# Hybrid S5 / RG-LRU encoder block: chunk-matrix sums by accumulating transfers, first norm by halves, embedding results in half tiles

## The chip, the cores and the metric

The kernel runs on one core of one Trainium2 chip. The metric is the device time of one execution in microseconds (us). Engines are named as in the profile: PE is the matrix engine (PEld its weight loads), DVE the vector engine, ACT the scalar engine, POOL the GpSimd engine, SP the sync engine, which here does nothing but issue transfers. SBUF is the on-chip memory, PSUM the memory that PE writes into, DRAM the memory of the chip's stacks.

## The reference

All data are float32, with 1024 positions and 1024 channels. Cut to what matters:

```
u = rms_norm(x, g_mix)                              # the first norm
u_a, x_b, gate_b, merge_a, merge_b = split(u @ w_in)       # 5 x 1024 columns
y_a  = u_a * s5_d
for d in (forward, backward):                       # S5: 64 groups of 16 channels, 64 complex states
    y_a += Re(C . scan(lam_bar, B_bar . u_a))
branch_a = gated(gelu(y_a)) @ w_a_out
branch_b = (rglru(conv(x_b)) * gelu(gate_b)) @ w_b_out
h = x + (sigmoid(merge_a)*branch_a + sigmoid(merge_b)*branch_b) @ w_o
v = rms_norm(h, g_ffn);  h = h + (silu(v @ w_ff_gate) * (v @ w_ff_up)) @ w_ff_down
h = h + sigmoid(rms_norm(h, g_ple) @ w_ple_gate) * (p @ w_ple_proj)   # the layer's embedding p
return rms_norm(h, g_final)
```

## The kernel before

**Numbers.** Every large product is made of three: each operand is split into a high part and a low part (ACT rounds the high part, DVE subtracts it from the original), and PE forms high x high, high x low and low x high.

**Start.** Eight tiles `xt[0..7]`, 128 positions by 1024 channels each, are loaded. `norm_pair` (line 190) takes two of them: ACT squares each tile and sums it (line 194) and takes the root (line 195), DVE does a Newton step on a 128x2 strip (`rstd_newton`) and scales both tiles (line 198). After two pairs `transposed_half` turns four tiles by PE (line 208) into PSUM, and from there ACT writes the high parts `xh` with the gain (line 213) and DVE the low parts `xl` (line 214), 512 columns at a time. Then come the next two pairs and the second half. The first products with `w_in` (`pi_u`, line 159) need all eight `xh`, `xl` of a half.

**Tables.** `s5_tables` then works out on DVE what the S5 recurrence needs, PE and ACT rearrange it, and it is stored to DRAM as `tab`. The first stretch of the S5 stage begins when the first of it is loaded back (`tb`).

**S5 stage.** Sixteen steps of four groups each. `s5_step(hb)` runs `s5_mid(hb)` (two scans on DVE with carries between them), then for step hb+2 `s5_mats` and `s5_front`, then `s5_out(hb)`. `s5_mats` builds two matrices of 128x1024 by `gen` (line 499): DVE forms two products into `t` and `u` (line 503) and adds them (line 505); `t` is called `mo` once and `mt` once, `u` is `mu`, a single buffer. From both PE forms `pk` (lines 516 and 519); ACT and DVE make the small tile `kt` of it, which goes through DRAM (`kk`, then `mr`) and comes back as `m0`. PE also transposes `mt` (`pmi`, line 536), ACT copies it to `mi` (line 538), and `s5_front` uses `mi` as weights for `pS` (line 551). `s5_out` needs `m0`, `mo` and the state `X` (`py`, lines 625 to 627). POOL issues no transfer; it only clears small strips of `carry`, `dzf` and `X` (lines 580, 583, 613).

**Fillers.** Beside the S5 steps stand projections: `inproj` is 48 products of 128x512 (line 159) for one block of 128 columns of `w_in`, one after most steps and two after every fourth. The twelve that are left come after the S5 stage, in the RG-LRU stage.

**Order.** Each engine runs its instructions in a fixed order. A planner sets that order when the program is built, from the order in the text (`tc.high_priority` moves a piece forward) and its own estimate of each duration; semaphores do the rest at run time. So an engine that waits for one instruction holds up everything planned behind it. Buffers are shared by tag: `ot(...)` hands out three tiles of 128x1024 (tag `o`), `act` forty of 128x512, and the tag `vt` four of 128x512.

**Embedding.** `embed_proj(m)` (line 1171) multiplies the embedding with `w_ple_proj` into two PSUM banks; ACT copies both to one tile `prj` from `ot` (line 1181) and one transfer stores it as `prd[m]` (line 1182). Around it run the first five hidden blocks' `head_group`s, whose result tile `hd` is also from `ot`, and the first `hidden_group`, whose second weight tile `fu` is from `ot` as well (line 1115, loaded at line 1047). Its first operands `rs` are sums of that weight tile (lines 1071 and 1072).

Of the kernel before, what the change touches and what calls it, by code (L numbers as in the profile page):

```python
# [8 lines left out]
F32 = mybir.dt.float32  # L9
F32R = mybir.dt.float32r  # L10
I32 = mybir.dt.int32
AF = mybir.ActivationFunctionType
# [3 lines left out]
MUL, ADD, SUB, MAX, MIN = ALU.mult, ALU.add, ALU.subtract, ALU.max, ALU.min  # L16
# [37 lines left out]
def block_kernel(tc, a, out):  # L54
    nc = tc.nc
    V, A, T, G = nc.vector, nc.scalar, nc.tensor, nc.gpsimd
    dma = nc.sync.dma_start
# [5 lines left out]
    cp = ctx.enter_context(tc.tile_pool(name="const", bufs=1))  # L63
# [11 lines left out]
    def psb(name):  # L75
        return pb.tile([128, 1024], F32, name=name, tag="pb")

    def ot(name):
        return op.tile([128, 1024], F32, name=name, tag="o")
# [12 lines left out]
    warm = cp.tile([128, 1], F32, name="warm")  # L92
# [19 lines left out]
    def r1(name, dt=F32R):  # L112
        return r1p.tile([128, S], dt, name=name, tag="r1", bufs=16)

    xh = [r1(f"xh{k}") for k in range(KT)]
    xl = [r1(f"xl{k}") for k in range(KT)]
# [4 lines left out]
    def slot(name, dt=F32, shape=None):  # L121
        return sp.tile(shape or [128, 1024], dt, name=name, tag="s", bufs=NS)
# [43 lines left out]
    xt, first_w = [], []  # L166
    for j in range(8):
        t = slot(f"x{j}")
# [8 lines left out]
    ss = cp.tile([128, 8], F32, name="ss")  # L177
    rs = cp.tile([128, 8], F32, name="rs")
    nt = cp.tile([128, 8], F32, name="nt")

    def rstd_newton(y, sq, t):

        V.reciprocal(y, y)
        V.tensor_scalar(t, sq, 1.0 / D, EPS, MUL, ADD)
        V.tensor_tensor(t, t, y, MUL)
        V.tensor_tensor(t, t, y, MUL)
        V.tensor_scalar(t, t, -0.5, 1.5, MUL, ADD)
        V.tensor_tensor(y, y, t, MUL)

    def norm_pair(q):  # L190
        qs = slice(q * 2, q * 2 + 2)
        for j in range(q * 2, q * 2 + 2):
            junk = ot("junk")
            A.activation(junk, xt[j], AF.Square, bias=warm, accum_out=ss[:, j:j + 1])
        A.activation(rs[:, qs], ss[:, qs], AF.Sqrt, bias=epsc, scale=1.0 / D)
        rstd_newton(rs[:, qs], ss[:, qs], nt[:, qs])
        for j in range(q * 2, q * 2 + 2):
            V.tensor_scalar(xt[j], xt[j], rs[:, j:j + 1], None, MUL)

    def transposed_half(h):  # L200

        cs = slice(h * 512, h * 512 + 512)
        ks = range(KT) if h == 0 else range(2)
        for k0 in range(0, KT, len(ks)):
            pt = [(psm if h == 0 and i % 2 else psb)("ptx") for i in range(len(ks) // 2)]
            for j in range(4):
                for k in ks:
                    T.transpose(pt[k // 2][:, (k % 2) * 512 + j * 128:(k % 2) * 512 + (j + 1) * 128],
                                xt[h * 4 + j][:, (k0 + k) * 128:(k0 + k + 1) * 128], ident)
            for k in ks:  # L210
                src = pt[k // 2][:, (k % 2) * 512:(k % 2) * 512 + 512]
                g = gmix[:, k0 + k:k0 + k + 1]
                A.activation(xh[k0 + k][:, cs], src, AF.Identity, scale=g)
                V.scalar_tensor_tensor(xl[k0 + k][:, cs], src, g, xh[k0 + k][:, cs].bitcast(F32), MUL, SUB)

    pv = psb("pv")
    T.transpose(pv[:, :8], grow, ident[:8, :8])
    V.tensor_copy(gmix, pv[:, :8])
    for h in range(2):
        norm_pair(2 * h)  # L220
        norm_pair(2 * h + 1)
        first_w[h] = split(first_w[h], [128, 8, 128], f"u{h}")
        transposed_half(h)


    vrows = cp.tile([128, 128], F32, name="vrows")
# [246 lines left out]
    ps = psb("ps_d")  # L473
# [10 lines left out]
    def st5(name, bufs, shape=None):  # L484
        return s5p.tile(shape or [128, 1024], F32, name=name, tag=name, bufs=bufs)

    def s5_mats(hb):
        tb = tabp.tile([128, MATW], F32, name="tb", tag="tb", bufs=2)
        dma(tb, tab[hb][:, 0:MATW])
        rb = tabp.tile([128, TABW - MATW], F32, name="rb", tag="trb", bufs=3)  # L490
        dma(rb, tab[hb][:, MATW:])

        def v8(o):
            return tb[:, o:o + 64].rearrange("p (d k) -> p d k", d=8)

        def v16(o):
            return tb[:, o:o + 128].rearrange("p (d k) -> p d k", d=8)

        def gen(o1, o2, q1, q2, name):
            t = st5(name, 3 if name == "mo" else 1, [128, 8, 16, 8])  # L500
            u = st5("mu", 1, [128, 8, 16, 8])
            for dst, o, q in ((t, o1, q1), (u, o2, q2)):
                V.tensor_tensor(dst, v8(o).unsqueeze(2).to_broadcast([128, 8, 16, 8]),
                                v16(q).unsqueeze(3).to_broadcast([128, 8, 16, 8]), MUL)
            V.tensor_tensor(t, t, u, ADD)
            return t

        mo = gen(O_LA, O_LB, O_K1, O_K2, "mo")
        t = gen(O_T1, O_T2, O_B1, O_B2, "mt")

        k1 = v16(O_K1)
        pk = psb("pk")
        bq = [t[:, q, :, 7 * (q // 4)] for q in range(8)]
        for q in range(8):
            d = q // 4
            T.matmul(pk[0:16, q * 128:q * 128 + 112], bq[q], mo[:, q, :, d:d + 7], start=True, stop=True)
        for g in range(4):
            for q in (g, 4 + g):
                T.matmul(pk[0:16, g * 128 + 112:(g + 1) * 128], bq[q], k1[:, q, :], start=(q < 4), stop=(q >= 4))
        kt = tabp.tile([16, 15, 4, 16], F32, name="kt", tag="kt", bufs=1)  # L520
        pkv = pk[0:16].rearrange("p (q n) -> p q n", q=8)
        A.copy(kt[:, 8:15].rearrange("p m g h -> p g h m"), pkv[:, 0:4, 0:112].rearrange("p g (h m) -> p g h m", m=7))
        A.copy(kt[:, 0:7].rearrange("p m g h -> p g h m"), pkv[:, 4:8, 0:112].rearrange("p g (h m) -> p g h m", m=7))
        V.tensor_tensor(kt[:, 7], ident[0:16, 0:16].unsqueeze(1).to_broadcast([16, 4, 16]),
                        dcol[:, hb * 4:hb * 4 + 4].unsqueeze(2).to_broadcast([16, 4, 16]), MUL)
        V.tensor_tensor(kt[:, 7], kt[:, 7], pkv[:, 0:4, 112:128], ADD)
        kd = kkd[hb]
        dma(kd.rearrange("p m n -> p (m n)"), kt.rearrange("p m g h -> p (m g h)"))
        mr = tabp.tile([128, 8, 4, 16], F32, name="mr", tag="mr", bufs=1)

        dma(mr.rearrange("p i g h -> p (i g h)"), bass.AP(kd.tensor, kd.offset, [[960, 16], [64, 8], [1, 512]]))
        m0 = tabp.tile([128, 4, 16, 8], F32, name="m0", tag="m0", bufs=3)
        A.copy(m0, mr.rearrange("p i g h -> p g h i"))
        pt = psb("pmi")
        for dg in range(8):
            T.transpose(pt[:, dg * 128:(dg + 1) * 128], t[:, dg].rearrange("p h j -> p (h j)"), ident)
        mi = st5("mi", MI, [128, 8, 128])
        A.copy(mi.rearrange("p d n -> p (d n)"), pt)  # L538
        return rb, m0, mi, mo
# [266 lines left out]
    tabp = tabp_cm.__enter__()  # L806
# [47 lines left out]
    for m in range(8):  # L854
        w = wload(a["s5_glu_w"][0][:, m * 128:(m + 1) * 128], f"gl{m}")
        ps = psm("pgl")
        gemm(ps, w, [x[0] for x in gp], [x[1] for x in gp])
        with hp():
            t = ot("glt")
            A.activation(t, ps, AF.Sigmoid, bias=vcol("s5_glu_b", m))  # L860
            g = ot("glg")
# [9 lines left out]
    for m in range(8):  # L871
        w = wload(a["w_a_out"][0][:, m * 128:(m + 1) * 128], f"ao{m}")
        ps = psm("pao")
        gemm(ps, w, [x[0] for x in yp], [x[1] for x in yp])
        with hp():
            t = ot("ta")
# [12 lines left out]
    qp = ctx.enter_context(tc.tile_pool(name="qp", bufs=1, reuse_waits="tile"))  # L889
# [8 lines left out]
    def half(n):  # L898
        return slice(n * 512, n * 512 + 512)
# [8 lines left out]
    for m in range(8):  # L908
        w = wload(a["w_b_out"][0][:, m * 128:(m + 1) * 128], f"bo{m}")
        ps = psm("pbo")  # L910
        gemm(ps, w, [x[0] for x in bp], [x[1] for x in bp])
        h, l = pair(f"mh{m}", F32R), pair(f"ml{m}", F32R)
        with hp():
            t, u = ot("tb"), ot("br")
# [26 lines left out]
    prd = [dram(f"prd{m}", [128, 1024]) for m in range(8)]  # L941
# [229 lines left out]
    def embed_proj(m):  # L1171

        if m % 4 == 0:
            with hp(HPW):
                wpp[0] = wload(a["w_ple_proj"][0][:, m * 128:m * 128 + 512], f"pp{m}")
        ps = [bank("ppj"), bank("ppj")]
        gemm(ps, wpp[0], pth, ptl, ms=slice((m % 4) * 128, (m % 4 + 1) * 128))
        yield
        t = ot("prj")
        for n in range(2):  # L1180
            A.copy(t[:, half(n)], ps[n])
        dma(prd[m], t)
        yield

    for n in range(2):
        acc = qp.tile([128, 512], F32, name="acc", tag="acc", bufs=2)
        for m in range(8):
# [8 lines left out]
            h = hpart(m, n)  # L1196
            A.copy(h, pt)
            ps = bank("pwo")
# [56 lines left out]
    for ib, nb in enumerate(BLOCKS):  # L1255
        fh, fl = [], []
        for ht in range(h0, h0 + nb):
            h, l = pair(f"fh{ht}", F32R), pair(f"fl{ht}", F32R)
            with hp(HPD):
                t = ot("hid")  # L1260
# [4 lines left out]
        if ib + 1 < len(BLOCKS):  # L1265
            for m in range(8):
                w = wload(wd[h0 * 128:(h0 + nb) * 128, m * 128:(m + 1) * 128], f"fd{h0}_{m}")
                ps = [bank("pfd"), bank("pfd")]
# [7 lines left out]
    for k in range(8):  # L1276
        t = r1(f"uh{k}")
# [3 lines left out]
    for n in range(2):  # L1281
        acc = qp.tile([128, 512], F32, name="acc", tag="acc", bufs=2)
        cs = slice(n * 512, n * 512 + 512)
        for m2 in range(4):
            w = wload(wd[(h0 - nb) * 128:h0 * 128, m2 * 256:(m2 + 1) * 256], f"fe{n}_{m2}")
            for mm in range(2):
                m = m2 * 2 + mm
                ps = bank("pfd")
# [33 lines left out]
    for n in range(2):  # L1322
# [3 lines left out]
        for m in range(8):  # L1326
            w = wload(a["w_ple_gate"][0][:, m * 128:(m + 1) * 128], f"pg{n}{m}")
            with hp(HPW):
                prj = act("prj")
                dma(prj, prd[m][:, cs])  # L1330
            ps = bank("ppg")
# [5 lines left out]
            t = qp.tile([128, 512], F32, name="vt2", tag="vt", bufs=4)  # L1337
# [4 lines left out]
            q = qp.tile([128, 512], F32, name="sqf", tag="vt", bufs=4)  # L1342
# [39 lines left out]
```

## Time and profile before

| | us |
|---|---|
| three runs | 1907.79, 1908.8, 1911.62 |
| median | 1908.8 |
| the profiled execution, its own time | 1907.41 |
| its span (first to last instruction) | 1905.2 |
| PE busy | 1841.4 (97%) |
| DVE busy | 1315.1 (69%) |
| ACT busy | 909.7 (48%) |
| POOL busy | 7.8 (0%) |

The span is what the profile pictures; 2.2 us lie around it. Busy time is a mean over stages: a stage is read by its own stretch of the span. Waits are listed as "engine, line, what waited <- who released it: total us, times, longest us".

### The profile page before, as it was taken

Reading aid. Unit: us, or ns where it says so; the run is one execution under the profiler, and the core shown is the slowest. Engines: PE = TensorE matmul, PEld = TensorE weight load, DVE = VectorE, ACT = ScalarE, POOL = GpSimd, SP = SyncE. Lnnn points to the kernel's source line nnn. Section 1 sums busy time; section 2 is a strip of 40 time slices with the busy share of each in tenths; the row PEclk is TensorE's granted clock in tenths of the full one; section 3 lists DMA queues with packets and bytes.
Section 4 is the critical chain, followed back from the end, with each engine's and each line's share of the span. In section 5 each row is a group of like instructions: output and inputs, shape, how many; then the busy total and the mean of one; then the engine's idle time right before and its main releaser. Section 6 shows DMA issues by size and latency. Waiting matters only on the chain.

```text
span 1905.2 us, 23270 instructions
## 1 busy us (share of the span) xinstructions
PE 1841.4 (97%) x8997; PEld 1532.0 (80%) x8997; DVE 1315.1 (69%) x1810; ACT 909.7 (48%) x1238; POOL 7.8 (0%) x60
## 2 busy tenths in 40 slices
PE   7999889988999999999999999999999999999998
PEld 6787777777788888878888887888888888888887
DVE  7517999999534779797444677867777774343875
ACT  6675666656555687865223454223232332122543
POOL 0000000000000000000000000000000000000000
PEclk8999999999999999999999999999999999999999
DMA  4795343433233356565746645422222264322433
GB/s 146 194 234 151 112 128 119 131 115 109 97 111 99 129 193 211 164 210 179 230 134 180 184 166 188 145 76 91 76 92 74 93 217 130 96 83 67 139 111 127
DMA packets 285855, 263.48 MB, mean 138 GB/s; under 512 B 32688, under 2 KB 244784, under 8 KB 285744
## 3 DMA queue, kind: packets, MB, share of 16 engines
q1 hardware_dynamic: 285744, 261.99, 44.2%
q8 instruction: 71, 1.16, 0.3%
q14 instruction: 40, 0.33, 0.1%
HBM read 185.86 MB, written 76.09 MB: 137 GB/s over the span
## 4 chain that ended last, share of the span: by engine, by line
PE 68%; DVE 2%; DMA 1%; ACT 1%; issue 1%; DVEq 0%; ACTq 0%
PE q L1060 22%; PE pfd L159 13%; PE pwo L159 5%; PE ppg L159 5%; PE pi_a L159 5%; PE pgl L159 5%; PE pg L159 4%; PE pbo L159 4%; PE pi_b L159 3%; PE pao L159 2%; PE ppj L159 1%; DMA ld_yb<-ybd 1%; DMA brd<-ta 1%; PE pfin L1312 0%; PE pxr L1195 0%
## 5 line engine op out<-in xcount | busy, mean ns | idle before, releaser
L1271 DVE TENSOR_TENSOR h<-h,pfd 128x512 f32<-128x512 f32 x48 | 32.6, 684 | 113.3 <-PE pfd L159 113.3
L982 ACT CAST s<-rs 128x512 fp32r<-128x512 f32 x44 | 27.2, 618 | 148.4 <-DVE rs L1072 148.4
L159 PE MATMUL pfd<-fh,wh_fd 128*128 128x512 f32 x288 | 88.7, 389 | 0.0
L159 PE MATMUL pfd<-fl,wh_fd 128*128 128x512 f32 x288 | 88.7, 389 | 0.0
L159 PE MATMUL pfd<-fh,wl_fd 128*128 128x512 f32 x288 | 88.6, 389 | 0.0
L134 ACT CAST wh_fd<-ws_fd 128x768 fp32r<-128x768 f32 x24 | 20.1, 835 | 122.1 <-PE pfd L159 121.4
L1060 PE MATMUL q<-xt2h,s 128*128 128x512 f32 x176 | 59.2, 398 | 4.3 <-ACT s L982 3.9
L159 PEld LDWEIGHTS pfd<-fl,wh_fd 128*128 128x128 f32 x288 | 54.1, 188 | 11.3
L159 PEld LDWEIGHTS pfd<-fh,wh_fd 128*128 128x128 f32 x288 | 54.1, 188 | 11.2
L159 PEld LDWEIGHTS pfd<-fh,wl_fd 128*128 128x128 f32 x288 | 54.1, 188 | 11.2
L1060 PE MATMUL q<-xt3h,s 128*128 128x512 f32 x176 | 57.7, 389 | 0.0
L1060 PE MATMUL q<-xt1h,s 128*128 128x512 f32 x176 | 57.7, 389 | 0.0
L1060 PE MATMUL q<-xt4h,a 128*128 128x512 f32 x176 | 57.7, 389 | 0.0
L1060 PE MATMUL q<-xb1h,s 128*128 128x512 f32 x176 | 57.7, 389 | 0.0
L551 PE MATMUL pS<-U,mi 128*128 128x128 f32 x256 | 32.6, 281 | 22.6 <-ACT mi L538 22.6
L551 PEld LDWEIGHTS pS<-U,mi 128*128 128x128 f32 x256 | 29.7, 191 | 28.9 <-ACT mi L538 28.5
L159 PE MATMUL pwo<-mh,wh_wo 128*128 128x512 f32 x128 | 51.5, 402 | 0.0
L159 PE MATMUL ppg<-uh,wh_pg 128*128 128x512 f32 x128 | 50.8, 397 | 0.0
L159 PE MATMUL pwo<-mh,wl_wo 128*128 128x512 f32 x128 | 50.1, 392 | 0.0
L159 PE MATMUL ppg<-uh,wl_pg 128*128 128x512 f32 x128 | 49.9, 390 | 0.0
L159 PE MATMUL ppg<-ul,wh_pg 128*128 128x512 f32 x128 | 49.8, 389 | 0.0
L159 PE MATMUL pwo<-ml,wh_wo 128*128 128x512 f32 x128 | 49.8, 389 | 0.0
(544 smaller groups left out, 5362.9 us busy)
## 6 DMA issues: line engine op xcount, KB each, us to landing
ws_fg<-in_w_ff_gate_dram SPq DMA_DIRECT2D x22, 512.0 KB, 4.2
fu<-in_w_ff_up_dram SPq DMA_DIRECT2D x22, 512.0 KB, 4.0
hid<-up SPq DMA_DIRECT2D x22, 512.0 KB, 3.4
hid<-hid SPq DMA_DIRECT2D x22, 512.0 KB, 4.6
ws_fd<-in_w_ff_down_dram SPq DMA_DIRECT2D x24, 384.0 KB, 3.5
ws_wo<-in_w_o_dram SPq DMA_DIRECT2D x16, 512.0 KB, 5.0
ws_pg<-in_w_ple_gate_dram SPq DMA_DIRECT2D x16, 512.0 KB, 3.9
tb<-tab SPq DMA_DIRECT2D x16, 384.0 KB, 3.1
```

Source lines behind the costliest of these rows:

```text
L134: A.copy(wh, st)
L159: T.matmul(pn_[:, sub], ww[:, k0 + k, ms], xn[:, sub], start=(first and i == 0), stop=(last and i == tot - 1))
L551: T.matmul(pS[:, q * 128:(q + 1) * 128], mi[:, q, :], rhs, start=True, stop=True)
L982: A.copy(h, raw)
L1060: T.matmul(ps, ww[:, k], xx, start=i == 0, stop=i == 11)
L1271: V.tensor_tensor(hres[m][:, half(n)], hres[m][:, half(n)], ps[n], ADD)
```

## The change

Four things change together.

1. `gen` no longer adds `u` to `t` on DVE. POOL issues a transfer that adds `u` into `t` while it writes (`accum_op=ADD`), SBUF to SBUF, 128x1024 float32. There are two of them for each of 16 steps. `mu` gets a second buffer, and to make room `kt` moves from a buffer of its own to a tile of tag `o`.
2. The first norm goes by four tiles: two are squared on ACT, two on DVE (`tensor_tensor_reduce`), then one root and one Newton step on a 128x4 strip, and of four tiles DVE scales three and ACT one.
3. The squares of the second half take their zero from a tile that DVE computes from `xl[4]` of the first half, so they come after it.
4. `prj` becomes two tiles of 128x512 of tag `vt`, each stored by a transfer of its own.

```diff
-    def norm_pair(q):
-        qs = slice(q * 2, q * 2 + 2)
-        for j in range(q * 2, q * 2 + 2):
+    def norm_half(h, start):
+
+        qs = slice(h * 4, h * 4 + 4)
+        for j in range(h * 4, h * 4 + 4):
             junk = ot("junk")
-            A.activation(junk, xt[j], AF.Square, bias=warm, accum_out=ss[:, j:j + 1])
+            if j % 2:
+                V.tensor_tensor_reduce(junk, xt[j], xt[j], 1.0, start, MUL, ADD, ss[:, j:j + 1])
+            else:
+                A.activation(junk, xt[j], AF.Square, bias=start, accum_out=ss[:, j:j + 1])
         A.activation(rs[:, qs], ss[:, qs], AF.Sqrt, bias=epsc, scale=1.0 / D)
         rstd_newton(rs[:, qs], ss[:, qs], nt[:, qs])
-        for j in range(q * 2, q * 2 + 2):
-            V.tensor_scalar(xt[j], xt[j], rs[:, j:j + 1], None, MUL)
+        for j in range(h * 4, h * 4 + 4):
+            if j % 4 == 3:
+                A.mul(xt[j], xt[j], rs[:, j:j + 1])
+            else:
+                V.tensor_scalar(xt[j], xt[j], rs[:, j:j + 1], None, MUL)
...
+    zeros = [warm, cp.tile([128, 1], F32, name="zero2")]
...
     for h in range(2):
-        norm_pair(2 * h)
-        norm_pair(2 * h + 1)
+        norm_half(h, zeros[h])
         first_w[h] = split(first_w[h], [128, 8, 128], f"u{h}")
         transposed_half(h)
+        if h == 0:
+
+            V.tensor_scalar(zeros[1], xl[4][:, 0:1].bitcast(F32), 0.0, None, MUL)
...
-            u = st5("mu", 1, [128, 8, 16, 8])
+            u = st5("mu", 2, [128, 8, 16, 8])
...
-            V.tensor_tensor(t, t, u, ADD)
+
+            G.dma_start(out=t.rearrange("p a b c -> p (a b c)"), in_=u.rearrange("p a b c -> p (a b c)"), accum_op=ADD)
...
-        kt = tabp.tile([16, 15, 4, 16], F32, name="kt", tag="kt", bufs=1)
+        kt = ot("kt")[0:16, 0:960].rearrange("p (m g h) -> p m g h", m=15, g=4)
...
-        t = ot("prj")
         for n in range(2):
-            A.copy(t[:, half(n)], ps[n])
-        dma(prd[m], t)
+            t = qp.tile([128, 512], F32, name="prj", tag="vt", bufs=4)
+            A.copy(t, ps[n])
+            dma(prd[m][:, half(n)], t)
```

## Rows read from the trace of the kernel before

**Rows 1.** The page's head.
```profile
span 1905.2 us, 23270 instructions
```

**Rows 2.** Busy time by stretch; then granted PE clock, transfer engines' share, GB/s.
```profile
0.00:24.00 24.00, 14.33 (x88) 12.78 (x88) 13.76 (x41) 17.06 (x29) 1.24 (x14) 0.88 0.75 251
24.00:50.00 26.00, 26.00 (x119) 21.17 (x120) 23.85 (x107) 13.82 (x18) 0.00 (x0) 0.92 0.19 57
50.00:150.00 100.00, 98.43 (x507) 80.22 (x506) 31.81 (x92) 63.17 (x120) 0.25 (x3) 1.00 0.88 218
150.00:510.00 360.00, 323.61 (x2141) 277.63 (x2140) 332.52 (x369) 223.10 (x308) 6.35 (x43) 1.00 0.38 117
510.00:1150.00 640.00, 636.17 (x2839) 524.77 (x2838) 421.26 (x422) 350.53 (x377) 0.00 (x0) 1.00 0.52 166
1150.00:1200.00 50.00, 45.72 (x194) 37.13 (x193) 35.41 (x58) 16.00 (x29) 0.00 (x0) 0.97 0.70 220
...
```

**Rows 3.** Waits from 150 to 510 us.
```profile
POOL X L613 <- PE py L627: 130.9, 14, 9.5
...
ACT rosw L481 <- DVE Y L610: 31.9, 16, 3.3
...
PE pS L551 <- ACT mi L538: 22.6, 14, 1.9
...
PE pk L516 <- DVE mt L505: 9.6, 11, 2.2
...
PE py L626 <- DVE X L614: 4.2, 3, 2.0
```

**Rows 4.** DVE's groups from 150 to 510 us: busy us, mean ns.
```profile
L586 DVE TENSOR_TENSOR_SCAN Y<-dzf,bb 128x1024 f32<-128x1024 f32 x16 | 36.5, 2281 | 0.6
...
L505 DVE TENSOR_TENSOR mt<-mt,mu 128x1024 f32<-128x1024 f32 x16 | 19.5, 1219 | 0.1
...
L505 DVE TENSOR_TENSOR mo<-mo,mu 128x1024 f32<-128x1024 f32 x16 | 19.2, 1198 | 0.0
```

**Rows 5.** One S5 step in order of time: start us, us.
```profile
297.40 1.22 DVE L505 TENSOR_TENSOR mt<-mt,mu 128x1024 f32<-128x1024 f32 x1
...
298.77 1.69 PE L516 MATMUL pk<-mo,mt 128*16 128x112 f32 x16 [0.96 <-DVE mt L505]
...
304.84 1.04 ACT L538 COPY mi<-pmi 128x1024 f32<-128x1024 f32 x1
...
305.94 2.05 PE L551 MATMUL pS<-U,mi 128*128 128x128 f32 x16 [1.65 <-ACT mi L538]
```

**Rows 6.** Transfers: KB of each, median us from issue to landing.
```profile
xbd<-oi_x SPq DMA_DIRECT2D x8, 512.0 KB, 2.6
...
tab<-tb_s SPq DMA_DIRECT2D x4, 512.0 KB, 6.7
...
kk<-kt SPq DMA_DIRECT2D x16, 60.0 KB, 1.9
```

**Rows 7.** The start in order of time.
```profile
5.09 1.15 ACT L194 ACTIVATE junk<-x,warm 128x1024 f32<-128x1024 f32 x1 [2.87 <-DMA x<-in_x_dram]
...
13.90 1.42 DVE L198 TENSOR_SCALAR x<-x,rs 128x1024 f32<-128x1024 f32 x2
...
17.00 0.67 ACT L213 ACTIVATE xh<-ptx,gmix 128x512 fp32r<-128x512 f32 x1
...
23.90 0.76 PE L159 MATMUL pi_u<-xh,wh_u 128*128 128x512 f32 x1
...
28.56 1.41 DVE L214 SCALAR_TENSOR_TENSOR xl<-ptx,gmix,xh 128x512 fp32r<-128x512 f32 x2 [1.07 <-ACT xh L213]
```

**Rows 8.** The first hidden group's start in order of time.
```profile
1151.77 0.38 SPq L1047 DMA_DIRECT2D fu<-in_w_ff_up_dram  x1
...
1157.77 0.68 DVE L1071 TENSOR_TENSOR rs<-fu 128x512 f32<-128x512 f32 x1
...
1160.36 0.50 PE L1060 MATMUL q<-xt2h,s 128*128 128x512 f32 x1 [3.86 <-ACT s L982]
```

## The prediction

> **What bounds the kernel now.** I start with the head of the page: the span is 1905.2 us [rows 1], the execution's own time 1907.4, the median of the three runs 1908.8. My sum is made against 1907.4; the median lies 1.4 above, and I add that at the end. PE is busy 97% of the span, so any gain must come out of the 3% in which it isn't, or out of work that is removed from PE. Nothing is removed from PE here.
>
> The second view is therefore busy time by stretch: where does PE stand idle [rows 2]? From 0 to 24 us it is busy 14.3; from 150 to 510, the S5 stage, 323.6 of 360, so 36.4 are idle; from 1150 to 1200 45.7, so 4.3 are idle. From 50 to 150 and from 510 to 1150 hardly anything is missing (1.6 and 3.8). The three parts of the change fall into the three stretches with gaps. The reader should also see DVE: 332.5 of 360 in the S5 stage, far above its mean of 69%, while ACT has 223. Only there is DVE an engine that matters.
>
> The third view, the waits of that stage, says at what PE stops [rows 3]: 22.6 us at `pS` for ACT's `mi`, 9.6 at `pk` for DVE's add, 4.2 at `py` for DVE's `X`. That sums to 36.4, the whole idle time. The largest isn't ACT's own fault: ACT itself waits 31.9 us for the scan `Y` of DVE before its `rosw` copies, and `mi` stands behind them in ACT's order. So most of PE's idle time in the stage goes back to DVE being late.
>
> **The S5 stage.** The change takes 32 adds from DVE: 16 of 1.219 and 16 of 1.198 us, 19.5 + 19.2 = 38.7 us [rows 4]. DVE goes from 332.5 to about 294 us of work, under PE's 323.6; PE becomes the busiest. I expect the wait at `pS` to fall from 22.6 to 5 and that at `py` from 4.2 to 2, since what they wait for is DVE's lateness, and 38.7 us of DVE is more than both. That leaves 7 of 26.8.
>
> The third wait is replaced by a new one. Now the add ends 1.2 us after it starts, and `pk` begins with it, after 0.96 us of waiting [rows 5]. After the change `pk`, and the transposes for `mi` behind it, wait for a transfer. No transfer of this kind is in the trace, and none issued by POOL. The nearest rows: a transfer of 512 KB lands 2.6 us after its issue in the best group and 6.7 in the worst, and 60 KB takes 1.9 [rows 6]. An accumulating transfer must read two tiles and write one. So it lands at the earliest with the best row (2.6), and at the latest when the part of the worst row that grows with size comes twice: 6.7 + (6.7 - 1.9) = 11.5. I take 5.5 as an estimate: a row between 2.6 and 6.7, with some of its data part doubled. Against the add of 1.2 the matrix is complete 4.3 us later (ends: 1.4 and 10.3).
>
> A delay costs PE only what isn't covered by filler products planned ahead of `pk`. The matrices are made two steps ahead of their use in `py`, so lateness there has room; but the order is fixed beforehand, and if the transfer lands later than the planner assumed, PE stands at `pk` and all behind it. Call the wait per step w. Today it is 9.6 / 16 = 0.6 us for the add. I take 0.8: nearest to that row, a little above it since landings of one size spread over 4 us. The ends are 0 (fully covered) and 10.3 (the latest landing, nothing covered). The stage's idle time becomes 7 + 16 x 0.8 = 19.8, so it gains 36.4 - 19.8 = 16.6 us.
>
> On POOL, the issue is queued among the clearings of `X`, `dzf` and `carry`. The clearing of `X` waits up to 9.5 us for PE's `py` [rows 3], and a transfer planned behind it waits as well. The other way about, a transfer that waits for DVE's second product holds back clearings; these idle for most of the stage today, so I price that at nothing; without that slack it is part of w. The second `mu` buffer is what keeps DVE from waiting for the landing. `kt` in the tag `o` shares three tiles with the fillers' results; at one `kt` and about one result per step I price it at nothing. If a tile were missing, a filler's result would be held up in PSUM by about the 1.9 us that `kk` takes to land [rows 6].
>
> The Trainium skill ("DMA: Bandwidth & Descriptors", section "Anatomy of one DMA — SWDGE (gpsimd) path") gives a transfer issued from GpSimd about 2.0 us plus its bytes at 436 GB/s; for 512 KB that is an estimate of 3.2 us, and with it w would rather be 0.5 and the gain some 5 us more. The page doesn't say that this holds for an accumulating one, and no row here shows one.
>
> **The start.** Now the squares begin at 5.1 us, each 1.15 on ACT; the second pair's scaling on DVE starts at 13.9 and takes 1.4; the first high part is written at 17.0; the first real product starts at 23.9, and the last low parts of the first half are being written at 28.6 to 30.0, because ACT and DVE have the second half's squares and scalings in between [rows 7]. With half the squares on DVE, four are done about 2.3 us sooner on ACT, one root and Newton step falls away from the path, and one scaling runs beside the others: I put the four scaled tiles at about 12 instead of 15.3. From there eight low parts of 0.7 us each, with nothing of the second half between them, end near 20 instead of 30. The second half, held back by the new zero, ends a few us sooner than now. PE gets its products earlier, but DVE takes up four squares. These aren't in the trace: at least as dear as an add (1.2), at most as a scan (2.28, [rows 4]); at 1.4 that is 5.6 us, less two scalings of 0.7, so +4.2 on an engine that is busy 23.9 of the 26 us from 24 to 50 [rows 2], when the S5 tables are worked out. So the bounds: -10 (all of what the low parts gain) and +4 (PE gains nothing and the S5 stage starts late). I take -4: PE starts sooner and puts the time into fillers ahead of the S5 stage. Part of this stretch runs below the full clock (granted 0.88 and 0.92 of 2.4 GHz, a mean of 1.2 and 2.4 GHz [rows 2]); that cost moves with the start and I leave it out.
>
> **The embedding.** PE stands 3.86 us at the first hidden group, for operands made from `fu`, which was issued at 1151.8 and reached DVE at 1157.8 [rows 8]. `fu` must have one of three tiles of tag `o`, which `hd` and `prj` hold until they are stored. With `prj` in `vt` the third tile is free several us sooner, and `fu` lands before PE needs it: -4. Ends: -4.3 (the stretch's whole gap) and +2 if four half tiles are too few: one is held for a copy and a landing of some 3 us, and then ACT and PE's banks wait. Eight more issues on SP are nothing beside that.
>
> **Sum.** -16.6 - 4 - 4 = -24.6; 1907.4 - 24.6 = 1882.8; on the median's scale 1884.2, and I say 1885.
>
> **The rivals.**
> *A. The sums land late* (chance 0.22). The mechanism: landing exceeds what the order allows, and PE, which now has the most work in the stage, waits at `pk` in all 16 steps. For it: PE stops there already for a 1.2 us add; POOL's queue can hold an issue for up to 9.5 us; in the stretch with 0.88 of the transfer engines busy, 512 KB took 6.7. Against it: in the S5 stage only 0.38 are busy [rows 2]. The change of time is 16 w + 7 - 36.4 - 8, so it is slower from w = 2.3 us on. At 3.5, it is +18.6: 1927 on the median's scale. The Trainium skill's "DMA: Bandwidth & Descriptors" (section "Issuing engines are not separate DMA queues") speaks for this: transfers from GpSimd run on the same engines as SP's and mix with them; the trace can't show it yet, since POOL issues none.
>
> *B. The S5 stage keeps its pace* (0.16). The wait at `pS` follows ACT's order (`kt` copies, then `mi`) and not DVE; what DVE gives up turns into DVE waiting, and the start's gain is lost at the first S5 product. Only the embedding's 4 us stay: 1905. For it: ACT's `mi` copy ends just before `pS` [rows 5]. Against it: ACT's own 31.9 us wait for DVE.
>
> *C. PE never stops in the stage* (0.14). w = 0 and both other waits gone: -36.4, the start -6, the embedding -4.3: -46.7, so 1862. Against it: in no stretch with DVE above 90% is PE full.
>
> The forecast has 0.48; its own range, with w from 0.2 to 1.5, is 1875 to 1896. What this kernel's measurements can tell from no change is about 0.2%, 3.8 us. Faster by more: 0.48 + 0.14 + half of B, 0.70. Within: the other half of B, 0.08. Slower: A, 0.22. For 8 in 10 I go from C's end, 1863, to 1922, which leaves out the worse half of A and a little of C.
>
> **What would show it.** In the trace after: no DVE add in `gen`, DVE at about 294 us in the S5 stage and PE at most 20 us idle there; the sum of waits at `pS` below 8; a wait of PE's `pk` on a transfer, with w to be read off; landing of POOL's transfers near 5.5 us; the first product before 20 us; no wait of 3.86 at the first hidden group. The prediction is wrong if `pk` waits more than 2.3 us per step, if landing is above 8 us, or if PE's idle time in the stage stays near 36 us with DVE below 300.

## The result and the profile after

The changed kernel takes 1966.4 us (median of four runs, 1963.3 to 1968.0) against 1908.4 for the kernel before: the ratio is 1.0298, with a 95% interval of 1.0280 to 1.0317. It is slower by 58 us where about 24 us faster was forecast, and outside the range of 1863 to 1922.

The head of the changed kernel's page and its busy line (compare [rows 1]; before, PE was busy 1841.4):

```profile
span 1963.5 us, 23335 instructions
PE 1863.0 (95%) x8997; PEld 1550.7 (79%) x8997; DVE 1289.2 (66%) x1773; ACT 909.2 (46%) x1232; POOL 35.6 (2%) x92
```

The span grew by 58.3. PE does the same 8997 products and is yet busy 21.6 us longer; its idle time grew by the other 36.7. So there are two losses: PE waits more, and the same work keeps it busy longer. Busy time by stretch (columns as in [rows 2]) says where:

```profile
...
150.00:510.00 360.00, 290.20 (x1842) 248.32 (x1841) 273.64 (x304) 198.62 (x274) 33.06 (x74) 0.91 0.60 152
1150.00:1200.00 50.00, 50.00 (x235) 41.20 (x234) 33.90 (x61) 23.89 (x41) 0.00 (x0) 1.00 0.44 144
150.00:250.00 100.00, 69.35 (x409) 58.62 (x408) 64.82 (x70) 43.31 (x56) 9.33 (x19) 0.80 0.57 141
250.00:560.00 310.00, 267.00 (x1691) 229.68 (x1690) 239.27 (x267) 180.52 (x253) 25.02 (x60) 0.96 0.56 144
```

In the S5 stage PE is busy 290.2 of 360 (323.6 before), and at a granted clock of 0.91 where it had 1.00. The worst part is its first 100 us: 69.35 at 0.80. In the kernel before the last two stretches read:

```profile
150.00:250.00 100.00, 90.17 (x598) 76.92 (x597) 90.90 (x98) 62.75 (x79) 1.32 (x9) 1.00 0.41 125
250.00:560.00 310.00, 283.45 (x1764) 242.11 (x1764) 257.54 (x285) 182.03 (x251) 5.03 (x34) 1.00 0.37 113
```

The embedding's gap is closed (50.00 of 50). DVE is busy 273.6 of 360, where the missing adds alone would leave 294: the stage now lasts longer (its last `py` ends at 547.7 us, before at 510.3), and a part of DVE's work has moved behind 510 us. The waits from 150 to 510 us, as [rows 3]:

```profile
...
PE pk L527 <- DMA mo<-mu: 25.1, 9, 7.3
DVE mu L513 <- DMA mt<-mu: 22.2, 8, 4.5
...
PE pS L562 <- ACT mi L549: 16.5, 9, 7.0
PE pk L527 <- DMA mt<-mu: 11.2, 2, 6.8
PE pi_x L159 <- ACT oi_x L680: 7.4, 4, 2.9
...
```

PE waits 36.3 us for the new transfers at `pk` (25.1 + 11.2; it waited 9.6 for the add [rows 3]), and DVE waits 22.2 for transfers to have read `mu`, in spite of its second buffer. A new line is a filler `pi_x` that waits for the copy of an earlier filler's result. The transfers themselves, as [rows 6], and their issues on POOL:

```profile
mo<-mu POOLq DMA_DIRECT2D x16, 512.0 KB, 4.5
mt<-mu POOLq DMA_DIRECT2D x16, 512.0 KB, 5.2
```
```profile
L516 POOL DMA_DIRECT2D mo<-mu x16 | 13.9, 871 | 80.1 <-DVE mo L513 39.7 <-DVE carry L613 19.3 <-DVE kt L535 13.5
```

They land 4.5 and 5.2 us after the issue begins, and an issue takes 0.87 us on POOL. The stage's first steps on PE, in order of time (start, us, idle before in brackets), and the stretch of the first `pk`:

```profile
167.96 3.15 PE L527 MATMUL pk<-mo,mt 128*16 128x112 f32 x16 [4.41 <-DMA mt<-mu]
180.01 3.11 PE L527 MATMUL pk<-mo,mt 128*16 128x112 f32 x16 [6.82 <-DMA mt<-mu]
...
197.88 1.22 PE L159 MATMUL pi_x<-xh,wh_in_x 128*128 128x512 f32 x2 [2.85 <-ACT oi_x L680]
```
```profile
167.90:171.20 3.30, 3.24 (x25) 2.69 (x26) 2.48 (x3) 0.00 (x0) 0.00 (x0) 0.50 0.80 159
```

The 16 `pk` products that took 1.69 us [rows 5] take 3.15 after such a wait, at a granted clock of 0.50: the lower of the two levels (1.2 GHz in place of 2.4). And from 168 to 198 us no filler stands between them, while before PE ran `pi_x` right behind the first `pk` and its transposes:

```profile
162.93 1.69 PE L516 MATMUL pk<-mo,mt 128*16 128x112 f32 x16 [2.17 <-DVE mt L505]
...
165.91 0.71 PE L159 MATMUL pi_x<-xh,wh_in_x 128*128 128x512 f32 x2
```

### The profile page after: what moved, and what is told of

The parts are those of the page before. It is cut to its first block, busy times and chain, and to the rows that moved or that the text cites. A ratio compares the mean times of both kernels' runs of the same rounds, so it can differ in the third digit from the quotient of the medians.

```text
span 1963.5 us, 23335 instructions
## 1 busy us (share of the span) xinstructions
PE 1863.0 (95%) x8997; PEld 1550.7 (79%) x8997; DVE 1289.2 (66%) x1773; ACT 909.2 (46%) x1232; POOL 35.6 (2%) x92
## 3 DMA queue, kind: packets, MB, share of 16 engines
q1 hardware_dynamic: 286896, 261.99, 42.4%
## 4 chain that ended last, share of the span: by engine, by line
PE 67%; DVE 2%; DMA 2%; ACT 2%; issue 1%; SPq 0%; ACTq 0%; DVEq 0%
PE q L1071 21%; PE pfd L159 12%; PE pwo L159 4%; PE ppg L159 4%; PE pi_a L159 4%; PE pi_b L159 4%; PE pbo L159 4%; PE pg L159 4%; PE pgl L159 3%; PE pao L159 2%; PE ppj L159 1%; DMA ld_yb<-ybd 1%; DMA brd<-ta 1%; PE pfin L1323 0%; PE pS L562 0%
## 5 line engine op out<-in xcount | busy, mean ns | idle before, releaser
L527 PE MATMUL pk<-mo,mt 128*16 128x112 f32 x256 | 33.3, 294 | 41.1 <-DMA mo<-mu 25.1
L527 PEld LDWEIGHTS pk<-mo,mt 128*16 128x16 f32 x256 | 26.8, 117 | 49.0 <-issue 42.5
L159 PEld LDWEIGHTS pfd<-fl,wh_fd 128*128 128x128 f32 x288 | 54.1, 188 | 11.3
L159 PEld LDWEIGHTS pfd<-fh,wl_fd 128*128 128x128 f32 x288 | 54.1, 188 | 11.2
L159 PEld LDWEIGHTS pfd<-fh,wh_fd 128*128 128x128 f32 x288 | 54.1, 188 | 11.2
L562 PE MATMUL pS<-U,mi 128*128 128x128 f32 x256 | 39.5, 319 | 21.5 <-ACT mi L549 20.3
L562 PEld LDWEIGHTS pS<-U,mi 128*128 128x128 f32 x256 | 36.7, 228 | 27.7 <-ACT mi L549 26.2
L513 DVE TENSOR_TENSOR mu<-tb 128x1024 f32<-128x1024 f32 x32 | 38.9, 1216 | 26.1 <-DMA mt<-mu 22.2
```

The costliest lines, as they stand in the source:

```text
L159: T.matmul(pn_[:, sub], ww[:, k0 + k, ms], xn[:, sub], start=(first and i == 0), stop=(last and i == tot - 1))
L562: T.matmul(pS[:, q * 128:(q + 1) * 128], mi[:, q, :], rhs, start=True, stop=True)
```

## The experiments

Each ratio is against runs of the kernel before on the same chip, with its 95% interval.

**First cut: which part.** One part alone in each run.

> Only the sums by accumulating transfers (with mu's second buffer and kt in the tag o). Theory 1, the sums alone did it: PE waits at pk for a landing some 2 to 7 us later than the order allows and its clock falls in the long waits; then this kernel is 55 to 70 us slower than before (1963 to 1978), since the embedding's gain of some 4 us is missing. Theory 2, the buffers moved did it: the same here, but then the run with the buffers alone is slower too. Theory 3, the later start of the S5 stage through the new norm did a good part: here only +35 to +50.

> Only the first norm by halves. Theory 1: the first product starts 1.4 us later and the S5 stage 3.5 us later in the changed kernel, so alone it costs +1 to +6 us (1909 to 1914). Theory 3 (it knocks the S5 stage out of its order): +15 us or more. As predicted before the change: -4.

> Only the embedding's results in half tiles. All theories: the stretch of 50 us around the first hidden group loses its 4.3 us of idle PE, so -3 to -5 us (1904). If the tag vt with its four tiles is too small, 0 to +2.

> DVE still adds; only mu gets a second buffer and kt moves to the tag o. Theories 1 and 3: within 3 us of before. Theory 2 (the buffers): +20 us or more.

The last one has only these two edits, with DVE still adding:

```diff
-            u = st5("mu", 1, [128, 8, 16, 8])
+            u = st5("mu", 2, [128, 8, 16, 8])
-        kt = tabp.tile([16, 15, 4, 16], F32, name="kt", tag="kt", bufs=1)
+        kt = ot("kt")[0:16, 0:960].rearrange("p (m g h) -> p m g h", m=15, g=4)
```

| run | median us | ratio (interval) |
|---|---|---|
| acc_only | 1970.3 | 1.0330 (1.0309 to 1.0351) |
| norm_only | 1907.2 | 0.9996 (0.9986 to 1.0006) |
| emb_only | 1902.5 | 0.9970 (0.9959 to 0.9982) |
| buf_only | 1937.1 | 1.0146 (1.0131 to 1.0161) |

The norm is worth nothing (its expectations, a gain of 4 or a loss, both missed), the embedding -5.5 us, and the S5 edits alone cost 62. Nearly half of that comes, as theory 2 had it, from making room: the buffers cost 29 us without any transfer.

**Second cut: which buffer, which sum.**

> The kernel before with only kt moved to the tag o; mu keeps one buffer, DVE still adds. The run with both buffer edits was +29 us. Theory K (the shared tag): kt now waits for one of three tiles of 128x1024 that the fillers' results hold until they are stored, and the order of the engines is another one; most of the +29 is here: 1930 to 1938, and ACT's kt copies or PE's products show waits on tiles of tag o. Theory M (the second mu buffer): the products for mu are placed earlier on DVE, ahead of the scans, and that is the cost; then this run is 1906 to 1912. If both count by half: about 1922.

> The accumulating transfers alone: mu keeps its single buffer and kt its own. Theory L (landing on the path): the next product into mu must wait for the landing of the last sum (about 5 us after the issue, less one product of 1.2 us), 16 to 32 times, and pk waits for it as in the changed kernel; DVE's waits at line 503 come to 60 us or more in the S5 stage and the time is 1955 to 1990, near the changed kernel's 1966 or above it. Theory A (the two costs simply add: +29 for the buffers, +33 for the transfers): without the buffers 1941, with DVE's waits at line 503 below 35 us.

> Both buffer edits, but only mo is summed by a transfer; mt is added by DVE. Theory L (landing on the path of pk and pmi): mo is summed first, and DVE's two products and the add for mt (3.6 us) cover most of the landing of 4.5 us, so this is close to the run with the buffers alone: 1934 to 1944, and PE's waits at pk on the transfer come to less than 10 us. Rival T (every such transfer costs alike, by its issue on POOL or by what it takes from others): half of the +33: 1954.

> Both buffer edits, but only mt is summed by a transfer; mo is added by DVE. Theory L: nothing covers the landing of mt (5.2 us), on which pk and the transposes for mi wait, so nearly the whole cost of the transfers is here: 1958 to 1972, with PE's waits at pk on the transfer above 20 us. Rival T: half of the +33: 1954, and as much for mo alone.

| run | median us | ratio (interval) |
|---|---|---|
| kto_only | 1937.9 | 1.0152 (1.0137 to 1.0167) |
| acc1 | 1957.9 | 1.0253 (1.0238 to 1.0268) |
| acc_mo | 1953.0 | 1.0228 (1.0213 to 1.0244) |
| acc_mt | 1947.9 | 1.0200 (1.0183 to 1.0217) |

Theory K holds in full: `kt` in the tag `o` costs 29 us by itself. (Theory L missed both mo and mt: alone, beside that `kt`, they cost 15 and 10 more than kto_only. acc_mo is where rival T put it, acc_mt below both theories.) The 29 us are lost at the stage's start: from 150 to 250 us PE is busy 18.2 us less than before and at a granted clock of 0.86, and behind that stretch it is busy as before (283.45):

```profile
150.00:250.00 100.00, 71.94 (x468) 61.05 (x467) 79.39 (x86) 49.43 (x64) 1.19 (x8) 0.86 0.32 95
250.00:560.00 310.00, 282.92 (x1767) 242.27 (x1766) 266.55 (x293) 188.38 (x257) 5.16 (x35) 0.99 0.38 117
```

ACT's order there explains it. First the kernel before, then kto_only:

```profile
161.30 2.01 ACT L669 COPY oi_x<-pi_x 128x1024 f32<-128x1024 f32 x1
165.16 0.97 ACT L522 COPY kt<-pk 16x448 f32<-16x448 f32 x1 [1.85 <-PE pk L519]
```
```profile
166.00 0.96 ACT L522 COPY kt<-pk 16x448 f32<-16x448 f32 x1 [4.03 <-PE pk L519]
175.34 0.94 ACT L522 COPY kt<-pk 16x448 f32<-16x448 f32 x1
189.82 2.06 ACT L669 COPY oi_x<-pi_x 128x1024 f32<-128x1024 f32 x1
```

Before, the filler results `oi_x` were copied at 150.4 and 161.3, ahead of the first `kt`; with the shared tag the first such copy comes at 189.8, behind three `kt`s. The products of the next fillers need a tile in PSUM, of which they have two, and these are free only after the copies; so PE has no filler to run between the `pk`s. On PE of kto_only:

```profile
171.65 3.15 PE L516 MATMUL pk<-mo,mt 128*16 128x112 f32 x16 [4.67 <-DVE mt L505]
191.93 1.22 PE L159 MATMUL pi_x<-xh,wh_in_x 128*128 128x512 f32 x2 [4.83 <-ACT oi_x L669]
```

In acc1 the transfers come without the shared tag but with one `mu`. Its time is theory L's (1955 to 1990), but DVE's waits for `mu` come to 32.4 us where L wanted 60, and so to theory A's (below 35). PE waits for the transfers in 15 of 16 steps, and DVE for their reading:

```profile
PE pk L516 <- DMA mt<-mu: 54.1, 15, 6.8
DVE mu L503 <- DMA mt<-mu: 21.8, 12, 5.2
DVE mu L503 <- DMA mo<-mu: 10.6, 9, 3.0
```

**Third cut: the tag repaired.** `kt` moves to the tag `mi`, whose two tiles serve only the S5 steps:

```diff
-        kt = ot("kt")[0:16, 0:960].rearrange("p (m g h) -> p m g h", m=15, g=4)
+        kt = s5p.tile([128, 1024], F32, name="kt", tag="mi", bufs=MI)[0:16, 0:960].rearrange("p (m g h) -> p m g h", m=15, g=4)
```

> Two buffers for mu, DVE still adds, and kt shares the tag mi (two tiles, used only inside the S5 steps) in place of the tag o. Theory F (fillers tied to the steps): kt in the tag o cost 29 us because the tag hands out its three tiles in the order of the text, so a filler's result could get none until the kt of the steps ahead of it in the text were stored, and PE ran out of fillers at the first three steps; without a tile shared with fillers the loss is gone: 1904 to 1914, and PE busy 150 to 250 us near the 90 of before. Rival G (any sharing of kt costs, or the second mu buffer with a changed order does): 1925 to 1940.

> The same buffers (two for mu, kt in the tag mi), and both sums by transfers. Theory L (PE waits at pk for the landing, and the granted clock falls in those waits): 1940 to 1958, with PE's and PEld's waits at pk on the transfer near 50 us, as with single buffers (1958), less what DVE no longer waits for mu. Rival D (the 1958 of the single buffer came from DVE waiting 32 us for mu to be read): 1905 to 1925.

> As the run before it, but the products and transfers of step hb+2 stand in the text ahead of the scans of step hb instead of behind them. Theory L: each landing then has the scans' time in front of pk, PE's waits at pk on a transfer fall below 15 us in the S5 stage, and with DVE's 38.7 us less work the time comes out under the kernel before: 1890 to 1908. Rival O (the order that the planner makes of it still puts mt's last product shortly before pk, or the first scan of each step is late instead): no better than the run before it, within 8 us of it.

> The same buffers, with the sums by an add on POOL in place of transfers: DVE is relieved by the same 38.7 us, but the sum is ready after one instruction, with no issue and no landing. Theory L: what counts is how late the sum is; if POOL's add of 128x1024 takes 2 to 3 us, the wait at pk is about half of that with transfers: 1910 to 1930. Rival T (what counts is that another engine has to be woken and waited for in a fixed order, not how long it takes): as with transfers, 1940 to 1958. If POOL's add slows DVE's work beside it, DVE's busy time in the S5 stage rises above 300 us.

| run | median us | ratio (interval) |
|---|---|---|
| buf_mi | 1906.6 | 0.9990 (0.9980 to 1.0000) |
| acc_mi | 1926.5 | 1.0096 (1.0081 to 1.0111) |
| early_mi | 1972.4 | 1.0336 (1.0321 to 1.0351) |
| pool_mi | 1964.3 | 1.0295 (1.0280 to 1.0310) |

Theory F is borne out by buf_mi: the same buffers, not shared with fillers, cost nothing. It differs from buf_only in the tag alone. Its first 100 us of the stage, and its wait at `pS`:

```profile
150.00:250.00 100.00, 91.13 (x600) 77.08 (x599) 91.21 (x97) 64.23 (x76) 1.31 (x9) 1.00 0.41 123
```
```profile
PE pS L551 <- ACT mi L538: 10.4, 14, 1.6
```

With room found this way the transfers cost 18 us (acc_mi), between the two theories and next to rival D's upper end. PE's waits there, 150 to 560 us, and two stretches:

```profile
PE pk L516 <- DMA mo<-mu: 16.4, 11, 2.5
PE pS L551 <- ACT mi L538: 12.4, 10, 2.5
PE pk L516 <- DMA mt<-mu: 7.5, 2, 4.7
PE py L626 <- DVE X L614: 4.7, 3, 2.3
```
```profile
150.00:250.00 100.00, 84.11 (x531) 70.80 (x530) 72.16 (x79) 54.99 (x68) 9.94 (x18) 0.95 0.66 163
250.00:560.00 310.00, 283.48 (x1760) 244.16 (x1759) 243.91 (x271) 184.12 (x256) 23.83 (x57) 0.98 0.59 152
```

The landing takes 23.9 us at `pk`, 1.5 a step. `pS` still waits 12.4 although 38.7 us of adds are gone from DVE, and in buf_mi it waits less, 10.4, with all adds still on DVE: its fall from 22.6 needs no relief of DVE. PE's busy time is 1853.4, 12.0 above before, for the same products.

early_mi failed its theory: earlier in the text is not earlier on the engines. It is 46 us slower than acc_mi, where rival O, whose mechanism this is, had allowed 8. The planner put `mo`'s products last on DVE, behind the first scan, and `pk` waits for their landing in 13 steps:

```profile
PE pk L517 <- DMA mo<-mu: 53.0, 13, 5.9
```

pool_mi is slower than either theory had it. One of POOL's two groups of adds, and three of DVE's groups beside them (150 to 560 us):

```profile
L505 POOL TENSOR_TENSOR mo<-mo,mu 128x1024 f32<-128x1024 f32 x16 | 45.2, 2827 | 55.8 <-DVE mo L503 35.2 <-issue 18.2 <-DVE kt L524 1.2
...
L503 DVE TENSOR_TENSOR mu<-tb 128x1024 f32<-128x1024 f32 x32 | 45.3, 1417 | 27.4 <-POOL mt L505 20.8 <-POOL mo L505 6.6
L564 DVE TENSOR_TENSOR rosw<-rosw,rb 128x1024 f32<-128x1024 f32 x16 | 24.1, 1505 | 10.4 <-ACT rosw L482 10.4
...
L602 DVE TENSOR_TENSOR_SCAN carry<-carry 128x64 f32<-128x64 f32 x16 | 21.8, 1362 | 0.1
```

In acc_mi, where DVE does the same work, these take 1214, 1224 and 286 ns; the small scan, 17.2 us in all, is the largest loss. DVE is busy 1320.0 us in pool_mi and 1285.4 in acc_mi: 34.6 us, nearly as much as the 38.7 of the adds, are lost to slower instructions beside POOL. (The Trainium skill's "SBUF — State Buffer", section "SBUF: two separate sides", has a port pair that DVE and POOL share and that one of them holds for a whole instruction, against DVE's instructions with two inputs in SBUF too. The longer means, 1362 ns in place of 286 above all, agree with it, though means don't show which port was held.) So pool_mi can't tell how much a shorter lateness is worth.

**Fourth cut: waiting or traffic.** dummy and dummy2 keep DVE's adds and issue as many transfers again into a tile that nobody reads (`kt` in the tag `mi`, one `mu`). dummy reads `mo` and `mt`; dummy2 reads `mo` alone, 28 times:

```diff
             V.tensor_tensor(t, t, u, ADD)
+            if name == "mo":
+                dmy[1:] = [t]
+            if hb >= 2:
+                G.dma_start(out=dmy[0], in_=dmy[1].rearrange("p a b c -> p (a b c)"), accum_op=ADD)
```

> DVE adds as before, kt in the tag mi, one mu buffer; beside it 32 transfers of the same size accumulate mo and mt into a tile that nothing reads, issued by POOL behind each add. The output is the reference's. Theory L (the wait for the landing is the cost): no gain and no loss, 1903 to 1912. Rival T (traffic and POOL's issues slow DVE, ACT or the loads): 1915 to 1928, with longer DVE or ACT instructions beside the transfers.

> As the run dummy, but both transfers of a step (28 in all, from the third step on) read mo, which is not written again for three steps, so that nobody but POOL waits for one. DVE adds; the output is the reference's. Theory L (waiting for a landing is the whole cost of the transfers): 1904 to 1912, with DVE's and ACT's instructions as long as without transfers. Rival T (traffic, or clearings held up in POOL's queue): 1918 to 1945, with waits of PE at py or of DVE's scans on POOL.

> Two mu buffers, kt in the tag mi, mo summed by a transfer and mt by DVE. mo has three tiles, mt one. Theory L: pk waits for both, so whichever sum comes last in DVE's order costs; where mo's products come behind mt's (as in the run with both, where PE waited 16.4 us for mo and little for mt) the cost is about the same as with both: 1918 to 1930. Rival S (the cost goes with the number of transfers): half, 1915. Rival H (mo's landing is covered by mt's products and add): 1895 to 1908, a gain from 19 us less work on DVE.

> The mirror: mt summed by a transfer, mo by DVE. Theory L with mo last in DVE's order: mt's landing is covered by mo's products and add, 1897 to 1910. Rival S: half, 1915. If mt's single tile (written again only after pmi has read it) makes DVE wait, 1918 to 1930, with waits of DVE at mt above 10 us.

| run | median us | ratio (interval) |
|---|---|---|
| dummy | 1950.6 | 1.0216 (1.0202 to 1.0230) |
| dummy2 | 1909.6 | 1.0005 (0.9995 to 1.0014) |
| acc_mo_mi | 1912.2 | 1.0018 (1.0009 to 1.0027) |
| acc_mt_mi | 1921.9 | 1.0062 (1.0048 to 1.0076) |

dummy fits neither of its theories and was no clean test: `mt` has one tile, and DVE had to wait for its reading.

```profile
DVE mt L504 <- DMA dmy<-mt: 50.7, 14, 4.7
```

dummy2 is clean: 28 such transfers, whose landing only POOL waits for, cost nothing, and DVE's products beside them stay at 1214 ns. So the cost of the transfers is waiting for them, not traffic. (The first two steps have none in dummy2, so for these it is argued.)

```profile
L510 POOL DMA_DIRECT2D dmy<-mo x28 | 24.2, 865 | 136.1 <-DVE mo L506 66.6 <-DVE carry L612 36.5 <-DMA dmy<-mo 29.6
```

One sum by transfer is cheaper: `mo` alone +3 us, just clear of no change; `mt` alone +12. Neither gains, and acc_mo_mi came out between its rivals S and H where theory L had 1918 to 1930. Its waits are what L said they would be:

```profile
PE pk L516 <- DMA mo<-mu: 21.7, 15, 2.5
```

That is almost the 23.9 of acc_mi for under a fifth of the cost, so the sum of the waits at `pk` is not the price. Other waits shrank as much: PE is idle 63.5 us of acc_mo_mi's span, 63.8 before. At `pk` none is longer than 2.5 us and the granted clock from 150 to 250 us stays at 1.00; in acc_mi the first is 4.7, the `pk` behind it takes 3.15 us, and that stretch has 0.95. acc_mt_mi missed theory L's 1897 to 1910. There PE waits for the transfer only 5.3 us, twice; the rest is spread over `py` and `pk` behind DVE, in an order of its own. DVE's waits at `mt`, the reason given for 1918 to 1930, aren't there. Why it is dearer than `mo` stays open.

**Last: the account, and a better version.** after_mi is the changed kernel with only `kt` in the tag `mi`. best is the kernel before with two `mu`, `kt` in `mi` and the half tiles.

> The changed kernel with kt in the tag mi in place of the tag o. Theory F (the shared tag is most of the loss, and ties the fillers just where the landings need them): the parts add now, 1908.8 + 18 - 5.5 + 0 = 1921, so 1916 to 1926, and PE busy 150 to 250 us above 82 (changed kernel 69). Rival P (the parts hinder each other in other ways, the new start above all): 1935 to 1960.

> No transfers: two mu buffers, kt in the tag mi, DVE adds, and the embedding's results through half tiles. If the two effects add (-1.7 and -5.5 us): 1901, ratio 0.996, faster than both kernels. If the buffers are worth nothing: 1903, as with the half tiles alone. If the other end of the S5 stage moves the embedding's weights against it: up to 1908.

after_mi takes 1918.2, ratio 1.0046 (1.0030 to 1.0063), as theory F had it: 48 of the 58 us lost come from where `kt` lies. best takes 1902.3, ratio 0.9966 (0.9953 to 0.9978), faster than both kernels by a little, but no faster than the half tiles alone.

## Why the prediction was wrong

**The failed step: "`kt` in the tag `o` ... I price it at nothing".** It cost 29 us alone and 48 in the changed kernel. I had counted tiles (one `kt` and one result per step, three tiles) and bounded the mishap by a 1.9 us store. The runs show that the order matters: fillers taken ahead of S5 steps, which is how PE fills the stage's start, were no longer taken ahead. (Whether a fourth tile in `o` would have helped was not run.) That the loss is larger beside the transfers fits: their waits of 4.4 and 6.8 us at the stage's start had no filler to cover them. No run shows this by itself.

**The S5 stage, "it gains 36.4 - 19.8 = 16.6 us".** This is the second step that failed: with the tag repaired the transfers cost 18 us. Three terms of it were wrong.

**w, the wait at `pk`.** I took 0.8 us a step, break-even 2.3. With the tag repaired it is 1.5 (23.9 / 16), with single `mu` 3.4 (54.1 / 16), in the changed kernel 2.3 (36.3 / 16). Rival A, which had 0.22, named this wait, but its sign came true by luck: by its own formula w = 1.5 is 13 us faster and 2.3 no change, and acc_mo_mi, with 21.7 us of such waits, is only 3 us slower. (The worst row for the landing was misread, too: 6.7 is the worst of [rows 6], but in the same view `x<-in_x_dram`, also 512 KB, has 8.1.)

**The wait at `pS`, "from 22.6 to 5", and `py` 2.** 12.4 and 4.7 in acc_mi. DVE's 38.7 us of adds are gone, but partly came back as waits of DVE for `mu` (16.0 us in acc_mi). And the premise, "what they wait for is DVE's lateness, and 38.7 us of DVE is more than both", fails: buf_mi, with all the adds, waits 10.4 at `pS`. With the landings, PE is idle 42.4 us from 150 to 560 in acc_mi, against 36.4 before and the 19.8 that I summed.

**The clock, "that cost ... I leave it out".** I left it out for the start alone and had no term for the S5 stage. There the granted clock was 1.00 before and falls with the longer waits. What that costs is an estimate from the rows above, busy time times the missing share of the clock: 69.35 x 0.20 + 267.00 x 0.04 = 24.6 us in the changed kernel, 84.11 x 0.05 + 283.48 x 0.02 = 9.9 in acc_mi. PE's busy time grew by 21.6 and 12.0; not all of such a growth need be the clock, since buf_mi, at 1.00 from 150 to 560 us and no slower than before, is busy 5.1 longer too. In acc_mi the clock's 9.9 is about as much as the growth of idle time (20.8 of span less 12.0, so 8.8).

**Rival C's reason against.** "In no stretch with DVE above 90% is PE full" misreads [rows 2]: from 24 to 50 us DVE is busy 23.85 and PE 26.00 of 26. Only C's chance hung on it.

**Right.** The landing: 5.5 estimated, 4.5 and 5.2 measured. The Trainium skill's "DMA: Bandwidth & Descriptors" (section "Anatomy of one DMA — SWDGE (gpsimd) path") would give 3.2 as an estimate; here the measurement decides. The same page of the Trainium skill (section "Issuing engines are not separate DMA queues") has the transfers of all engines run on the same 16 transfer engines and interleave. dummy2 shows no cost of that, at 0.57 of them busy. The second `mu` as what keeps DVE from waiting: with one, the transfers cost about 30 us more (ratios of acc1 and acc_mi), though two don't take all the wait away. The embedding: -4 forecast, -5.5 measured. `fu` is issued earlier, and PE's wait of 3.86 us [rows 8] is gone; emb_only:

```profile
1147.70 0.38 SPq L1047 DMA_DIRECT2D fu<-in_w_ff_up_dram  x1
1151.89 0.69 DVE L1071 TENSOR_TENSOR rs<-fu 128x512 f32<-128x512 f32 x1 [1.32 <-DMA fu<-in_w_ff_up_dram]
```

**The start, -4 forecast, 0 measured.** The four scaled tiles were to be there at 12 us and a first product before 20. In the changed kernel the scalings end at 16.1 and the first product comes at 25.3, later than before (15.3 and 23.9 [rows 7]). The squares were to be done 2.3 us sooner; ACT has its two by 8.7, but DVE starts its two only at 9.1, behind a copy that waits for PE, and ends them at 11.6:

```profile
8.99 0.17 DVE L226 COPY gmix<-pv 128x8 f32<-128x8 f32 x1 [8.99 <-PE pv L225]
9.13 1.28 DVE L196 CUSTOM_DVE_ANT_0 junk<-x,warm 128x1024 f32<-128x1024 f32 x1
...
13.99 2.08 DVE L205 TENSOR_SCALAR x<-x,rs 128x1024 f32<-128x1024 f32 x3
14.88 5.74 PE L215 MATMUL ptx<-ident,x 128*128 128x128 f32 x32 [5.93 <-DVE x L205]
25.29 0.47 PE L159 MATMUL pi_u<-xh,wh_u 128*128 128x512 f32 x1 [4.67 <-DVE xl L221]
```

One root for four tiles needs all four sums. By pairs, as before, the first pair went ahead, and its transposes ran while the second got its root and was scaled:

```profile
10.94 3.44 PE L208 MATMUL ptx<-ident,x 128*128 128x128 f32 x16 [2.51 <-DVE x L198]
```

That lead I had overlooked. And the eight low parts of the first half, which were to end near 20 with nothing of the second half between them, end at 32.3, with squares of the second half among the last three. norm_only is none the slower for it, and its trace shows where the loss is paid back. The S5 stage's first product on DVE starts 2.8 us later than before (157.4 against 154.6), but the last `py` 2.6 us earlier (507.3 against 509.9), since PE waits less at `pk` (9.6 before [rows 3]):

```profile
PE pk L526 <- DVE mt L515: 3.4, 5, 1.5
```

Why that wait is shorter isn't shown.

**The sum, redone.** Transfers with free buffers +18, half tiles -5.5, norm 0: +12.5, against +10 measured in after_mi. The shared tag adds 48 to that: the 58 us of the changed kernel. Of the 83 us between forecast (-24.6) and result, the tag is 48 and the S5 stage's sum 34.6 (from -16.6 to +18). (The start adds 4, the embedding takes off 1.5, and 2.5 don't add up.)

## What to carry to other kernels

A scratch tile moved into a shared tag is not priced by its bytes or its holding time: ask whose turn it takes, and whether that user was being run ahead of its place in the text. A sum by transfer trades 1.2 us of an engine for about 5 us of lateness; it is free where nobody waits (dummy2), and could pay only where the consumer stands that far behind in the order that is really made, which has to be read, not assumed from the text; no run here shows it paying. Less work on an engine shortens a wait only if the order turns it into an earlier result. Where PE is the bound, price a new wait with the clock, and look at the longest waits and not at their sum alone: in acc_mi the slower clock cost about as much (an estimated 9.9 us) as the added idle time.

## What the runs showed of the hardware

- After waits of 4.4 to 6.8 us, PE's next products ran at about half speed (3.11 to 3.15 us in place of 1.69, the first at a granted clock of 0.50); after acc_mo_mi's waits of at most 2.5 us the stage's first `pk` took 1.69. The changed kernel's first 100 us of the stage had a granted clock of 0.80.
- An accumulating transfer of 512 KB from SBUF to SBUF lands in 4.5 to 5.2 us (medians of the changed kernel; 6.0 and 5.6 in early_mi) and takes 0.87 us to issue on POOL. DVE's products of 128x1024 beside it don't slow down (1214 ns in dummy2, 1210 before).
- An add of 128x1024 on POOL takes 2.5 to 2.8 us (POOL's spans are rough) and slows DVE's instructions beside it (1417 ns in place of 1214, 1505 in place of 1224, and a scan of 128x64 1362 in place of 286).
